# Weight stream in half chunks, and output banks emptied by units of their own, in a two-block fp32 transformer kernel

## The chip, the core and the metric

One core of a Trainium2 chip runs the whole program. Its engines work side by side, each through its own queue in order: TensorE (PE) multiplies, with weight loads (PEld) that overlap; VectorE (DVE) and ScalarE (ACT) work on SBUF and on the eight PSUM banks into which PE writes; GpSimd (POOL) does a little; SyncE (SP) issues the DMAs that bring weights from HBM. The metric is the device time of one execution in microseconds (us), lower is better.

## What is computed

Two layers of block 1 and two of block 2 on 256 tokens of width 1024, batch 1, all in float32. The reference, cut (in block 1 the attention is a differential one and a block one side by side; with 256 tokens the block one is plain causal attention):

```python
    for i in range(DEPTH):                      # block 1, DEPTH = 2
        h = rms_norm(x, ln_attn_g[i])
        dq, dk, dv, mq, mk, mv = jnp.split(h @ w_in[i], cuts, axis=-1)
        ...
        x = x + jnp.concatenate([y_diff, y_moba], axis=-1) @ w_out[i]
        x = x + conv_ffn(rms_norm(x, ln_ffn_g[i]), w_up[i], conv_w[i], conv_b[i], w_down[i])

def conv_ffn(h, w_up, conv_w, conv_b, w_down):
    u = causal_dwconv(h @ w_up, conv_w, conv_b)
    g, up = jnp.split(u, 2, axis=-1)
    return (jax.nn.silu(g) * up) @ w_down

    for l in range(L):                          # block 2, L = 2
        x = x + 0.5 * swiglu(rms_norm_2(x, ffn1_norm[l]), ffn1_w_gate[l], ffn1_w_up[l], ffn1_w_down[l])
        h = rms_norm_2(x, mix_norm[l])
        proj = h @ w_in[l] + b_in[l]
        q, k, v, f_logit, xr, gr, g_attn, g_rnn = jnp.split(proj, SPLIT_POINTS, axis=-1)
        ...
        y_attn = forgetting_attention(q, k, v, log_f) @ w_o_attn[l]
        xr = causal_depthwise_conv(xr, conv_w[l], conv_b[l])
        yr = rg_lru(xr, lru_w_a[l], lru_b_a[l], lru_w_x[l], lru_b_x[l], lru_lambda[l]) * jax.nn.gelu(gr)
        y_rnn = yr @ w_o_rnn[l]
        merged = jax.nn.sigmoid(g_attn) * y_attn + jax.nn.sigmoid(g_rnn) * y_rnn
        x = x + merged @ w_out[l]
        x = x + 0.5 * swiglu(rms_norm_2(x, ffn2_norm[l]), ffn2_w_gate[l], ffn2_w_up[l], ffn2_w_down[l])
```

The hidden width of every FFN is 2816, which is 22 tiles of 128.

## The kernel before

**Arithmetic.** A float32 value is split into a high part (a copy rounded to the multiplier's float32r) and a low part (the rest), and a product is made of high x high, low x high and high x low. Activations are kept transposed, 128 features by 256 tokens, with the high and the low part side by side in one tile of 512 columns. `mm2` is thus a pair of matmuls: the high weights against all 512 columns, and the low weights against the 256 high ones, added onto the first half of the same bank. An output tile fills one bank, whose two halves (`hi`, `lo`) are added when it is emptied.

**Weight stream.** All weights come in one list of chunks in the order of use, mostly 1 MB each (128 x 2048). SP brings a chunk into one of `NRAW` = 3 raw buffers; ACT writes its high part `wh` and DVE its low part `wl`, in `NP` = 4 pieces of 128 x 512, into one of `RING` = 3 buffers. ACT or DVE waits with a new chunk's first piece until PE is done with the chunk that held the buffer. `fill` and `urgent` put these pieces between other work; `next_chunk` hands a finished chunk to the matmuls and sets `st["done"]`, from which `h_open` sees which buffers may be written.

**Order.** The program is straight-line, and each engine runs its instructions as they were emitted. After nearly every pair of matmuls the emitter calls `substep`, which puts in weight pieces and lets background work advance. Background work is a list of Python generators, called units: a unit does a step on ACT or DVE, names the tile that it waits for, and goes on once an `Estimate` of each engine's time says that the tile is there. Units spawned with `front=True` come first and may run further ahead of PE (`CAPF` 4500 against `CAP` 1400 ns). The estimate only sets the order; on the chip semaphores hold it.

**FFN.** `proj2` makes two output tiles (gate and up) from one chunk: 16 pairs of matmuls into two banks `mm`. The unit `evac_swiglu` or `evac_conv` empties them into a tile `u` (ACT copies one half of each bank, DVE adds the other), scales by the norm's `rstd`, does silu and product (the conv one also four DVE taps into `y`), and writes the split hidden tile `as`. `ffn_order` sets where the down matmuls come: groups of four hidden tiles, the first half of the outputs beside the ups with a lag (4 tiles for the conv FFN, 2 for swiglu), then the second half. A half's last group runs output by output, and each finished output goes to `boundary` (x is updated, its square is added up on POOL for the next norm).

**Mix 2** runs the steps of `MIX2`: projections q, k, v, x, a, n, the block-diagonal gates G, then r0 to r3, n2, n3 (from the normed input `hS`), A0 to A3 (attention output), R0 to R3 (recurrence output `sp`), O0 to O3. The recurrence is in `lru_unit` (ACT exp, square, ln, exp; DVE products and scans into `z`), one for each of four tiles. `gelu_unit` empties the banks of r0 to r3 with a bias into `ge`, waits until all four recurrences are done, and then makes gelu, the product with `z`, and the split `sp`. It stands behind the `lru_unit`s in the list. `ya_unit` and `yr_unit` empty the banks of A and R and multiply by the gates `sg`.

Of the kernel before, what the change touches and what calls it, by code (L numbers as in the profile page):

```python
# [25 lines left out]
NG = -(-NF // 4)  # L26
NBLK = 41
# [40 lines left out]
class Estimate:  # L68
# [9 lines left out]
    def key(self, x):  # L78

        w = self.wide.get(x.name)  # L80
        return x.name if w is None else (x.name, 4 * x.offset // w)

    def cost(self, eng, op, out, ins, kw):
# [12 lines left out]
        if eng == "pool":  # L96
            return 149.0 + 2.1 * w
# [47 lines left out]
def kernel(ctx: ExitStack, tc: tile.TileContext, t: dict):  # L145
# [34 lines left out]
    def phase_chunks():  # L180
        for l in range(L):
            wo = t["w_out"]
            at = {"dq0": 0, "dq1": 1, "mq0": 2, "mq1": 3, "dv0": 4, "mv0": 5}
            for step in MIX1.split():
                if step[1] == "o":
                    stream.append(wo[l, 2 * (step[0] == "m") + int(step[2])])
                else:
                    stream.extend(t["w_p1"][l, at[step], i] for i in range(2))
            ffn_chunks(t["w_up"], t["w_down"], l, 4)
        for l in range(L):  # L190
# [3 lines left out]
            for step in MIX2.split():  # L194
                if step == "q0":
                    stream.append(t["w_qf"][l])
                elif step == "G":
                    stream.append(t["w_g"][l])
                elif step in PAIRS:
                    stream.extend(t["w_p2"][l, PAIRS.index(step), i] for i in range(2))  # L200
                elif step[0] == "O":
                    stream.append(half_rows(t["w_out2"][l], *divmod(int(step[1]), 2)))
                elif step[0] in "AR":
                    stream.append(t[{"A": "w_oa", "R": "w_or"}[step[0]]][l, int(step[1])])
                else:
                    stream.append(wi[l, base[step[0]] + int(step[1])])
            ffn_chunks(t["w_gu2"], t["w_d2"], l, 2)

    def half_rows(w, half, g):

        v = w[2 * g:min(2 * g + 2, w.shape[0])].rearrange("c p (k m) -> p c k m", k=2)
        return v[:, :, :, half * 512:(half + 1) * 512]

    def ffn_order(lag):
# [3 lines left out]
        for j in range(NF):  # L218
            yield "up", j
            while left and 4 * left[0] + 3 + lag <= j:  # L220
                yield "dn", (0, left.pop(0))
        for g in left:
            yield "dn", (0, g)
        for g in [NG - 1, *range(NG - 1)]:
            yield "dn", (1, g)

    def ffn_chunks(u, d, l, lag):
        for what, j in ffn_order(lag):
            stream.append(u[l, j] if what == "up" else half_rows(d[l], *j))
# [10 lines left out]
    NRAW = 3  # L240
    RING = 3
    NP = 4
# [7 lines left out]
    def issue_dma(parts=1, also=None):  # L250
# [16 lines left out]
        T["dma"] = max(T["dma"], T["dve"] if c >= NRAW else 0.0) + 2900.0  # L267
# [7 lines left out]
    def piece_h():  # L275
        c, p = divmod(st["h"], NP)
        if p == 0:
            Hs[c] = wpool.tile([P, wide(c)], F32R, tag="wh", bufs=RING, name=nm("wh"))
            Ls[c] = wpool.tile([P, wide(c)], F32R, tag="wl", bufs=RING, name=nm("wl"))
            est.wide[Hs[c].name] = est.wide[Ls[c].name] = wide(c)  # L280
# [18 lines left out]
    def fill():  # L299

        issue_dma()
        while h_open() and st["h"] - st["l"] < 2 * NP:
# [9 lines left out]
    def urgent():  # L312

        if st["l"] < min((st["use"] + 1) * NP, NCHUNK * NP):
# [88 lines left out]
    for x in X:  # L403
        est.wide[x.name] = 4 * S
# [7 lines left out]
    for c in range(2):  # L412
        issue_dma(NP, lambda i: i % 2 == 0 and nc.sync.dma_start(X[2 * c + i // 2], t["x"][2 * c + i // 2]))
    for p in range(4):
        est.R[X[p].name, 0] = est.R[X[p].name, 1] = T0 - 500.0 + 2200.0 * p
    est.R[raws[0].name], est.R[raws[1].name], T["dma"] = T0 + 200.0, T0 + 4600.0, T0 + 5500.0
    nc.sync.dma_start(cst, t["cst"])
    T["dma"] += 1400.0
    issue_dma()
# [25 lines left out]
    def mm3(out, lh, ll, rh, rl, start, stop):  # L445
        pe.matmul(out, lh, rh, start=start, stop=False, skip_group_check=True)
        pe.matmul(out, lh, rl, start=False, stop=False, skip_group_check=True)
        pe.matmul(out, ll, rh, start=False, stop=stop, skip_group_check=True)

# [108 lines left out]

    def mm2(b, lh, ll, x, start, stop):
# [4 lines left out]
    def proj2(R):  # L564

        h, l_ = next_chunk(None)
        h3 = h.rearrange("p (k c) -> p k c", k=KT)
        l3 = l_.rearrange("p (k c) -> p k c", k=KT)
        wait_for(lambda: bank_any(2))
        bs = [bank("mm") for _ in range(2)]  # L570
        for k in range(KT):
            for m in range(2):
                ms = slice(m * P, (m + 1) * P)
                mm2(bs[m], h3[:, k, ms], l3[:, k, ms], R.both(k), k == 0, k == KT - 1)
# [4 lines left out]
    def add_parts(t, bs):  # L579

        yield W("act", *bs)
        for m in range(2):
            act.activation(as2(t)[:, m], lo(bs[m]), AF.Copy)
        yield W("dve", t)
        for m in range(2):
            dve.tensor_add(as2(t)[:, m], hi(bs[m]), as2(t)[:, m])
            unbank()

    def add_bias(t, bs, cols):

        yield W("act", *bs)
        for m in range(2):
            act.activation(as2(t)[:, m], hi(bs[m]), AF.Identity, bias=cols[m])
        yield W("dve", t)
        for m in range(2):
            dve.tensor_add(as2(t)[:, m], lo(bs[m]), as2(t)[:, m])
            unbank()

    def vproj(R):

        h, l_ = next_chunk(None)
        h3 = h.rearrange("p (k c) -> p k c", k=KT)
        l3 = l_.rearrange("p (k c) -> p k c", k=KT)
        w = h3.shape[2]
# [4 lines left out]
        for k in range(KT):  # L609
            for m in range(2):  # L610
                ms = slice(m * P, (m + 1) * P)
                mm3(o[m], R.high(k)[:, ms], R.low(k)[:, ms], h3[:, k], l3[:, k],
# [5 lines left out]
    def vpair(R):  # L618
# [3 lines left out]
        for half in range(2):  # L622
            h, l_ = next_chunk(None)
            h3 = h.rearrange("p (k c) -> p k c", k=KT // 2)
            l3 = l_.rearrange("p (k c) -> p k c", k=KT // 2)
            for kk in range(KT // 2):
                k = half * (KT // 2) + kk
                for tt in range(2):
                    xh, xl = R.high(k)[:, tt * P:(tt + 1) * P], R.low(k)[:, tt * P:(tt + 1) * P]
                    last = k == KT - 1  # L630
                    pe.matmul(bs[tt], xh, h3[:, kk], start=k == 0, stop=False, skip_group_check=True)
                    substep()
                    pe.matmul(bs[tt], xl, h3[:, kk], start=False, stop=False, skip_group_check=True)
                    pe.matmul(bs[tt], xh, l3[:, kk], start=False, stop=last, skip_group_check=True)
                    if not (last and tt):
                        substep()
        return bs

    def down(acc, R, first, last, after=None):

        h, l_ = next_chunk(None)
        h3 = h.rearrange("p (k c) -> p k c", k=2)
        l3 = l_.rearrange("p (k c) -> p k c", k=2)

        def one(k, m):
            ms = slice(m * P, (m + 1) * P)
            mm3(as2(acc[m // 2])[:, m % 2], h3[:, k, ms], l3[:, k, ms], R.high(k), R.low(k),
                first and k == 0 and m % 2 == 0, last and k == 1 and m % 2 == 1)

        if not last:  # L650
            for k in range(2):
                for mh in range(2):
                    for m in range(4 * mh, 4 * mh + 4):
                        one(k, m)
                        substep()
        else:
            for p in range(4):
                for k in range(2):
                    for m in (2 * p, 2 * p + 1):
                        one(k, m)  # L660
# [6 lines left out]
    def down2(acc, R, ks, half_, first, last, after):  # L667

        h, l_ = next_chunk(None)
# [44 lines left out]
    def ffn(N, evac, scale, N2, lag, mul):  # L714
# [3 lines left out]
        for what, j in ffn_order(lag):  # L718
            if what == "up":
                spawn(evac(N, mul(R), j, A.tiles))  # L720
                substep()
            else:
                half_, g = j
                ks = range(4 * g, min(4 * g + 4, NF))
                wait_for(lambda: all(A.tiles[k] is not None for k in ks))
# [4 lines left out]
                down2(acc[half_], A, ks, half_, first, g == NG - 1 - half_, boundary(scale, N2))  # L730
# [10 lines left out]
    def evac_swiglu(N, bs, j, tiles):  # L741
        u = blk("u")
        yield from add_parts(u, bs)
        while N.rstd is None:
            yield POLL
        yield W("dve", u, N.rstd)
# [7 lines left out]
    def make_evac_conv(l):  # L754
        def evac(N, bs, j, tiles):
            u = blk("u")
            yield from add_parts(u, bs)
            while N.rstd is None:
                yield POLL
            yield W("dve", u, N.rstd)  # L760
# [21 lines left out]

    class Box:
        def __init__(self):
            self.ready = False
# [515 lines left out]
    def xr_unit(b, j, l, R):  # L1301

        x2 = blk("xr")
        yield from add_bias(x2, b, [v1(("bin", l), 24 + 2 * j + m) for m in range(2)])
# [39 lines left out]
    def sig_unit(b, cols, box, ready):  # L1344

        box.s = blk("sg")
        yield from add_bias(box.s, b, cols)
        while not ready():
            yield POLL
        yield W("act", box.s)  # L1350
# [323 lines left out]
```

## Time and profile before

| what | value |
|---|---|
| median of 3 runs (lowest to highest) | 1907.61 us (1906.86 to 1914.71) |
| the profiled execution: its time, its span | 1908.4 us, 1906.6 us |
| busy: PE, PEld, DVE, ACT, POOL | 97%, 85%, 81%, 67%, 4% |
| chain that ended last: PE, DVE, ACT, DMA | 89%, 4%, 4%, 2% |
| weights and data read from HBM | 336 MB, 177 GB/s over the span |

A matmul's end is modelled, and matmuls overlap, so the starts are to be read, not the lengths. A pair of `proj2` begins every 0.35 us. Where PE waits, the trace prints the wait in brackets with the instruction that ended it. The granted clock of a stretch (PEclk) is 1.00 at 2.4 GHz and 0.50 at 1.2 GHz. Since PE is at work for nearly the whole span, time can come from its waits, and from the stretches after them in which the clock is lower.

### The profile page before, as it was taken

How to read it: one execution, taken by the hardware profiler on the slowest of the kernel's cores; microseconds unless marked ns; L12 is line 12 of the kernel's file. 1: busy time of each engine (PE TensorE's matmuls, PEld its weight loads, DVE VectorE, ACT ScalarE, POOL GpSimd, SP SyncE). 2: the span in 40 equal slices, each digit the busy share in tenths (PEclk: the TensorE clock that was granted, in tenths of full speed). 3: DMA queues.
4: the chain of work that ended last, by engine and by line, in shares of the span. 5: the costliest groups of instructions: out<-in, count | busy, mean ns of one | idle time of the engine just before them, and what ended most of it. 6: DMA issues, size and time to landing. Idle time of an engine off the chain costs nothing.

```text
span 1906.6 us, 29974 instructions
## 1 busy us (share of the span) xinstructions
PE 1854.1 (97%) x10742; PEld 1618.0 (85%) x10742; DVE 1551.5 (81%) x3389; ACT 1283.8 (67%) x3211; POOL 68.9 (4%) x98
## 2 busy tenths in 40 slices
PE   8899999999999999999998999999999999899999
PEld 6788788888888888888887888888889888788888
DVE  6889997887989777778978977678777897888775
ACT  6777675877766665567787665566556778866653
POOL 3000000001000100000000100010001000000000
PEclk9999999999999999999999999999999999899999
DMA  9435455434545655474454555455556454455543
GB/s 260 142 128 181 173 172 204 147 124 163 181 160 166 209 193 185 153 258 164 145 192 168 190 182 193 164 199 192 198 169 241 155 177 162 169 180 199 193 159 132
DMA packets 79156, 339.59 MB, mean 178 GB/s; under 512 B 7020, under 2 KB 8084, under 8 KB 48288
## 3 DMA queue, kind: packets, MB, share of 16 engines
q1 hardware_dynamic: 77408, 330.20, 51.3%
q0 software_dynamic: 1456, 7.47, 1.4%
q8 instruction: 84, 1.38, 0.3%
q14 instruction: 64, 0.52, 0.1%
q10 hardware_dynamic: 144, 0.02, 0.0%
HBM read 336.30 MB, written 1.36 MB: 177 GB/s over the span
## 4 chain that ended last, share of the span: by engine, by line
PE 89%; DVE 4%; ACT 4%; DMA 2%; issue 1%; SPq 0%; ACTq 0%
PE mm L112 50%; PE acc L112 23%; PE mv L112 12%; DMA raw<-in_w_p 2%; DVE wl L112 2%; PE av L112 1%; ACT wh L112 1%; PE s L112 1%; PE qt L112 1%; PE pt L112 1%; DVE y L112 1%; ACT r L112 1%; ACT th L112 1%; DVE z L112 0%; DVE yc L112 0%
## 5 line engine op out<-in xcount | busy, mean ns | idle before, releaser
L112 DVE TENSOR_TENSOR wl<-raw,wh 128x512 fp32r<-128x512 f32 x1272 | 812.6, 679 | 142.3 <-ACT wh L112 133.0
L112 ACT ACTIVATE wh<-raw 128x512 fp32r<-128x512 f32 x1272 | 701.0, 618 | 146.4 <-PE acc L112 85.4
L112 PE MATMUL mm<-xs,wh 128*128 128x512 f32 x2112 | 742.6, 396 | 11.4 <-ACT as L112 8.4
L112 PE MATMUL mm<-xs,wl 128*128 128x256 f32 x2112 | 592.5, 281 | 0.0
L112 PEld LDWEIGHTS mm<-xs,wh 128*128 128x128 f32 x2112 | 397.7, 188 | 104.3 <-ACT as L112 9.0
L112 PEld LDWEIGHTS mm<-xs,wl 128*128 128x128 f32 x2112 | 401.0, 190 | 0.2
L112 PE MATMUL acc<-as,wh 128*128 128x512 f32 x1056 | 372.3, 396 | 6.6 <-DVE as L112 6.5
L112 PE MATMUL acc<-as,wl 128*128 128x256 f32 x1056 | 297.0, 281 | 0.0
L112 PE MATMUL mv<-wh,xs 128*128 128x512 f32 (+2 forms) x832 | 255.1, 384 | 0.2 <-ACT wh L112 0.2
L112 PEld LDWEIGHTS acc<-as,wh 128*128 128x128 f32 x1056 | 199.5, 189 | 53.1 <-DVE as L112 7.9
L112 ACT ACTIVATE u<-mm 128x256 f32<-128x256 f32 x264 | 95.5, 383 | 171.3 <-PE mm L112 171.1
L112 PEld LDWEIGHTS acc<-as,wl 128*128 128x128 f32 x1056 | 201.2, 191 | 0.0
L112 PE MATMUL mm<-hS,wh 128*128 128x512 f32 x512 | 184.2, 403 | 16.7 <-DVE ge L112 16.7
L112 DVE TENSOR_TENSOR u<-mm,u 128x256 f32<-128x256 f32 x264 | 100.4, 422 | 102.7 <-ACT u L112 102.6
L112 PEld LDWEIGHTS mv<-wh,xs 128*128 128x128 f32 x832 | 149.5, 189 | 26.8 <-ACT wh L112 0.7
L112 PE MATMUL mv<-wl,xs 128*128 128x512 f32 (+2 forms) x416 | 156.3, 376 | 0.2 <-DVE wl L112 0.2
L112 PE MATMUL mm<-hS,wl 128*128 128x256 f32 x512 | 144.4, 282 | 0.0
L112 PEld LDWEIGHTS mm<-hS,wh 128*128 128x128 f32 x512 | 98.0, 191 | 39.7 <-issue 17.3
L112 POOL TENSOR_TENSOR sq<-sq,sq 128x256 f32<-128x256 f32 x70 | 55.7, 796 | 1592.6 <-ACT sq L112 1590.8
L112 PEld LDWEIGHTS mm<-hS,wl 128*128 128x128 f32 x512 | 98.2, 192 | 0.1
L112 ACT ACTIVATE as<-u 128x256 fp32r<-128x256 f32 x88 | 36.3, 417 | 82.2 <-DVE u L112 82.2
L112 DVE TENSOR_TENSOR u<-u,rstd 128x512 f32<-128x512 f32 x132 | 90.3, 686 | 0.0
(208 smaller groups left out, 2262.8 us busy)
## 6 DMA issues: line engine op xcount, KB each, us to landing
raw<-in_w_gu SPq DMA_DIRECT2D x88, 1024.0 KB, 4.9
raw<-in_w_up SPq DMA_DIRECT2D x44, 1024.0 KB, 4.8
raw<-in_w_d SPq DMA_DIRECT2D x88, 512.0 KB, 4.8
raw<-in_w_p SPq DMA_DIRECT2D x42, 1024.0 KB, 5.1
raw<-in_w_in SPq DMA_DIRECT2D x34, 1024.0 KB, 4.8
raw<-in_w_down SPq DMA_DIRECT2D x44, 512.0 KB, 4.6
raw<-in_w_out SPq DMA_DIRECT2D x8, 1024.0 KB, 4.8
raw<-in_w_oa SPq DMA_DIRECT2D x8, 1024.0 KB, 4.9
```

The costliest lines, as they stand in the source:

```text
L112: f(*a, **k)
```

## The change

The list `stream` holds half chunks of 128 x 1024 (512 KB). A piece is still 128 x 512, so a half has two (`NP` 2). There are 7 raw buffers of a half and 5 buffers of converted halves, in place of 3 and 3 whole ones. `k_chunks` hands the halves to the matmuls one after another. Down groups have two hidden tiles, one half chunk each; the last two of the second half of the outputs run together. `urgent` looks two halves ahead.

A new unit, `summed`, empties the two banks of a `proj2` as its first and only step and is spawned with `front=True`; `evac_swiglu`, `evac_conv`, `xr_unit`, `sig_unit`, `gelu_unit`, `ya_unit` and `yr_unit` start from its tile in place of the banks. The bias is added by ACT to the half that ACT reads. The seven additions of squares of the first norm run on DVE, not on POOL. POOL's cost in the estimate changes, and the x tiles, the constants and the first raw halves are issued in another mix at the start. The matmuls are the same in number and shape.

```diff
-NG = -(-NF // 4)
-NBLK = 41
+NG = NF // 2
+NBLK = 43
...
-            return 149.0 + 2.1 * w
+            return 738.0 + 1.22 * w
         if op == "reciprocal":
             return 69.0 + 6.25 * w
...
         for j in range(NF):
             yield "up", j
-            while left and 4 * left[0] + 3 + lag <= j:
-                yield "dn", (0, left.pop(0))
+            while left and 2 * left[0] + 1 + lag <= j:
+                yield "dn", (0, (left.pop(0),))
         for g in left:
-            yield "dn", (0, g)
-        for g in [NG - 1, *range(NG - 1)]:
-            yield "dn", (1, g)
+            yield "dn", (0, (g,))
+        for g in range(NG - 2):
+            yield "dn", (1, (g,))
+        yield "dn", (1, (NG - 2, NG - 1))
...
-    NRAW = 3
-    RING = 3
-    NP = 4
+    NRAW = 7
+    RING = 5
+    NP = 2
...
-        if len(stream[c].shape) == 4:
-            rv = r.rearrange("p (c k m) -> p c k m", k=2, m=512)
-            for i in range(rv.shape[1]):
-                nc.sync.dma_start(rv[:, i], stream[c][:, i])
+        if len(stream[c].shape) == 3:
+            nc.sync.dma_start(r.rearrange("p (k m) -> p k m", k=2), stream[c])
         else:
             for i in range(parts):
                 if also:
                     also(i)
                 nc.sync.dma_start(r[:, i * w:(i + 1) * w], stream[c][:, i * w:(i + 1) * w])
-        T["dma"] = max(T["dma"], T["dve"] if c >= NRAW else 0.0) + 2900.0
+        T["dma"] = max(T["dma"], T["dve"] if c >= NRAW else 0.0) + 1450.0
         est.R[r.name] = T["dma"] + 2200.0
         return True
...
 
-        if st["l"] < min((st["use"] + 1) * NP, NCHUNK * NP):
+        if st["l"] < min((st["use"] + 2) * NP, NCHUNK * NP):
...
         else:
-            pool.tensor_add(N.ss[0], N.ss[0], sq)
+            (dve if N is norms[0] else pool).tensor_add(N.ss[0], N.ss[0], sq)
             N.ss = (N.ss[0], N.ss[1] + 1)
 
...
 
+    def k_chunks(n=KT, c=2):
+
+        per = n // c
+        for i in range(c):
+            h, l_ = next_chunk(None)
+            h3 = h.rearrange("p (k c) -> p k c", k=per)
+            l3 = l_.rearrange("p (k c) -> p k c", k=per)
+            for j in range(per):
+                yield i * per + j, h3[:, j], l3[:, j]
...
+    def summed(name, bs, cols=None):
+
+        x = Box()
+        x.t = blk(name)
+
+        def unit():
+            yield W("act", *bs)
+            for m in range(2):
+                if cols is None:
+                    act.activation(as2(x.t)[:, m], lo(bs[m]), AF.Copy)
+                else:
+                    act.activation(as2(x.t)[:, m], lo(bs[m]), AF.Identity, bias=cols[m])
+            yield W("dve", x.t)
+            for m in range(2):
+                dve.tensor_add(as2(x.t)[:, m], hi(bs[m]), as2(x.t)[:, m])
+                unbank()
+            x.ready = True
+
+        spawn(unit(), front=True)
+        return x
...
-    def down2(acc, R, ks, half_, first, last, after):
-
-        h, l_ = next_chunk(None)
-        h3 = h.rearrange("p (k c) -> p k c", c=512)
-        l3 = l_.rearrange("p (k c) -> p k c", c=512)
-
-        def one(i, m):
+    def down2(acc, R, groups, half_, first, last, after):
+
+        n = 2 * len(groups)
+
+        def one(i, m, h, l_):
             ms = slice(m * P, (m + 1) * P)
-            mm2(acc[m], h3[:, i, ms], l3[:, i, ms], R.both(ks[i]), first and i == 0, last and i == len(ks) - 1)
+            mm2(acc[m], h[:, ms], l_[:, ms], R.both(2 * groups[i // 2] + i % 2), first and i == 0, last and i == n - 1)
 
         if not last:
-            for i in range(len(ks)):
+            for i, h, l_ in k_chunks(n, len(groups)):
                 for m in range(4):
-                    one(i, m)
+                    one(i, m, h, l_)
                     substep()
         else:
+            w = list(k_chunks(n, len(groups)))
             for m in range(4):
-                for i in range(len(ks)):
-                    one(i, m)
-                    if i < len(ks) - 1:
+                for i, h, l_ in w:
+                    one(i, m, h, l_)
+                    if i < n - 1:
...
-    def gelu_unit(b, j, l, R):
-        ge = blk("ge")
-        yield from add_bias(ge, b, [v1(("bin", l), 32 + 2 * j + m) for m in range(2)])
-        while R.nh < 4:
-            yield POLL
+    def gelu_unit(x, j, l, R):
+        while not x.ready or R.nh < 4:
+            yield POLL
+        ge = x.t
         yield W("act", ge, R.h[j])
         fn(ge, ge, AF.Gelu_apprx_tanh)
         yield W("dve", ge)
```

Units `evac_swiglu`, `evac_conv`, `xr_unit`, `sig_unit`, `ya_unit` and `yr_unit` change as `gelu_unit` does.

ACT's order in the first layer of block 2, from the end of the gates to r3 (`ge<-mm` empties a bank of r0 to r3; `th<-th` are the ln and exp of a recurrence; `wh` is a weight piece). Before:

```order
L112 ACTIVATE wh_11068<-raw_10908 128x512 x4
L112 ACTIVATE th_10813<-th_10813,tiny 128x512
L112 ACTIVATE th_10813<-th_10813 128x512
L112 ACTIVATE th_10835<-th_10835,tiny 128x512
L112 ACTIVATE th_10835<-th_10835 128x512
L112 ACTIVATE wh_11119<-raw_10971 128x512 x4
L112 ACTIVATE th_10865<-th_10865,tiny 128x512
L112 ACTIVATE th_10865<-th_10865 128x512
L112 ACTIVATE ge_10952<-mm_10888,vec 128x256
L112 ACTIVATE ge_10952<-mm_10889,vec 128x256
L112 ACTIVATE ge_11006<-mm_10953,vec 128x256
L112 ACTIVATE ge_11006<-mm_10954,vec 128x256
```

The same place after the change:

```order
L112 ACTIVATE wh_11486<-raw_11246 128x512 x2
L112 ACTIVATE th_11425<-r_11424,sp_105 128x256 x2
L112 ACTIVATE wh_11509<-raw_11283 128x512
L112 ACTIVATE ge_11514<-mm_11448,vec 128x256
L112 ACTIVATE ge_11514<-mm_11449,vec 128x256
L112 ACTIVATE wh_11509<-raw_11283 128x512
L112 ACTIVATE th_11467<-r_11466,sp_105 128x256 x2
L112 ACT_TABLE_LOAD
L112 ACTIVATE r_11372<-r_11372,sp_105 128x256 x2
L112 ACTIVATE z_11544<-r_11372 128x512
L112 ACTIVATE wh_11552<-raw_11309 128x512 x2
L112 ACTIVATE ge_11574<-mm_11518,vec 128x256
```

The first bank of r0 is emptied ahead of the table load and the recurrence's exp, where it stood behind three recurrences' ln and exp.

DVE's order at the same layer's A steps and the start of R0 (`ya<-mm` empties the banks of an A step, `sp<-ge` makes the input of R0). Before, where A0's banks come behind all of `sp`:

```order
L112 TENSOR_TENSOR sp_11281<-ge_11063,sp_11281 128x256
L112 TENSOR_TENSOR sp_11315<-ge_11063,sp_11315 128x256
L112 TENSOR_TENSOR sp_11286<-ge_11118,sp_11286 128x256
L112 TENSOR_TENSOR sp_11321<-ge_11118,sp_11321 128x256
L112 TENSOR_TENSOR sg_11273<-mm_11209,sg_11273 128x256
L112 TENSOR_TENSOR sg_11273<-mm_11210,sg_11273 128x256
L112 TENSOR_TENSOR wl_11297<-raw_11129,wh_11296 128x512 x4
L112 TENSOR_TENSOR ya_11338<-mm_11276,ya_11338 128x256
L112 TENSOR_TENSOR ya_11338<-mm_11277,ya_11338 128x256
```

After the change, where the banks are those of A3, directly ahead of R0:

```order
L112 TENSOR_TENSOR sp_12061<-ge_11574,sp_12061 128x256
L112 TENSOR_TENSOR sp_12072<-ge_11574,sp_12072 128x256
L112 TENSOR_TENSOR ya_12079<-mm_12010,ya_12079 128x256
L112 TENSOR_TENSOR ya_12079<-mm_12011,ya_12079 128x256
L112 TENSOR_TENSOR ge_11637<-ge_11637,z_11633 128x512
L112 TENSOR_TENSOR ge_11696<-ge_11696,z_11686 128x512
L112 TENSOR_TENSOR sg_11047<-ya_12007,sg_11047 128x512
L112 TENSOR_TENSOR sg_11236<-ya_12079,sg_11236 128x512
L112 TENSOR_TENSOR sp_12088<-ge_11637,sp_12088 128x256
L112 TENSOR_TENSOR sp_12091<-ge_11637,sp_12091 128x256
```

The last four `sp` moved from ahead of A0's banks to behind A3's banks and four products.

DVE's order in the first conv FFN, at the eleventh up (`u<-mm` empties its banks, `y<-u` are taps of the convolution). Before:

```order
L112 SCALAR_TENSOR_TENSOR y_2432<-u_2353,vec,y_2432 128x254
L112 TENSOR_TENSOR wl_2427<-raw_2317,wh_2426 128x512 x4
L112 TENSOR_TENSOR as_2484<-y_2409,as_2484 128x256
L112 TENSOR_TENSOR y_2432<-y_2432 128x256
L112 TENSOR_TENSOR u_2418<-mm_2354,u_2418 128x256
L112 TENSOR_TENSOR u_2418<-mm_2355,u_2418 128x256
L112 TENSOR_TENSOR u_2476<-mm_2421,u_2476 128x256
L112 TENSOR_TENSOR u_2476<-mm_2422,u_2476 128x256
```

After:

```order
L112 SCALAR_TENSOR_TENSOR y_2606<-u_2471,vec,y_2606 128x255
L112 SCALAR_TENSOR_TENSOR y_2606<-u_2471,vec,y_2606 128x254
L112 SCALAR_TENSOR_TENSOR y_2606<-u_2471,vec,y_2606 128x255
L112 SCALAR_TENSOR_TENSOR y_2606<-u_2471,vec,y_2606 128x254
L112 TENSOR_TENSOR u_2631<-mm_2565,u_2631 128x256
L112 TENSOR_TENSOR u_2631<-mm_2566,u_2631 128x256
L112 TENSOR_TENSOR wl_2571<-raw_2418,wh_2570 128x512 x2
L112 TENSOR_TENSOR wl_2598<-raw_2450,wh_2597 128x512 x2
```

The banks of the up are emptied ahead of the weight pieces and one up at a time, where two ups' banks were emptied behind four pieces.

## Rows read from the trace of the kernel before

**Rows 1.** The profile's page: span, and busy time of each engine.

```profile
span 1906.6 us, 29974 instructions
PE 1854.1 (97%) x10742; PEld 1618.0 (85%) x10742; DVE 1551.5 (81%) x3389; ACT 1283.8 (67%) x3211; POOL 68.9 (4%) x98
```

**Rows 2.** PE's waits: for what; us in total, times, longest us.

```profile
PE mm L112 <- DVE ge L112: 16.7, 2, 8.4
PE qt L112 <- DVE qn L112: 9.5, 1, 9.5
PE mm L112 <- ACT as L112: 8.4, 2, 4.2
PE acc L112 <- DVE as L112: 6.5, 2, 3.3
PE mm L112 <- ACT wh L112: 2.0, 2, 1.0
PE st L112 <- POOL sq L112: 1.3, 1, 1.3
```

**Rows 3.** Windows: stretch and length, busy us of each engine, PEclk, DMA share, GB/s.

```profile
142.40:301.90 159.50, 150.54 (x854) 131.00 (x852) 149.07 (x314) 111.75 (x249) 2.35 (x3) 0.99 0.52 172
651.00:812.00 161.00, 161.00 (x930) 142.07 (x929) 124.21 (x247) 100.53 (x223) 4.31 (x6) 1.00 0.53 177
...
1600.00:1650.00 50.00, 41.64 (x243) 36.70 (x242) 34.57 (x66) 44.35 (x94) 0.00 (x0) 0.90 0.43 147
...
1012.20:1025.00 12.80, 12.80 (x65) 11.14 (x66) 10.77 (x24) 10.27 (x21) 0.00 (x0) 0.87 0.16 48
...
212.00:218.00 6.00, 5.00 (x19) 4.30 (x20) 5.83 (x14) 2.55 (x6) 0.00 (x0) 0.72 0.50 175
...
302.00:308.00 6.00, 6.00 (x25) 5.18 (x26) 5.81 (x13) 4.18 (x10) 1.49 (x2) 0.72 0.55 176
```

**Rows 4.** Timeline of PE between r3 and n2: start, length, instruction, [idle before].

```profile
1002.96 0.40 PE L112 MATMUL mm<-hS,wh 128*128 128x512 f32 x1
...
1003.31 0.40 PE L112 MATMUL mm<-hS,wh 128*128 128x512 f32 x1
...
1012.19 0.76 PE L112 MATMUL mm<-hS,wh 128*128 128x512 f32 x1 [8.37 <-DVE ge L112]
```

**Rows 5.** Timeline of ACT at the same place: the banks of r0 to r3.

```profile
1007.27 3.01 ACT L112 ACTIVATE ge<-mm,vec 128x256 f32<-128x256 f32 x8
```

**Rows 6.** DVE's groups from 975 to 1060 us: busy us, mean ns | idle before.

```profile
L112 DVE TENSOR_TENSOR ya<-mm,ya 128x256 f32<-128x256 f32 x8 | 3.0, 423 | 3.2 <-ACT ya L112 3.2
L112 DVE TENSOR_TENSOR sp<-ge,sp 128x256 fp32r<-128x256 f32 x8 | 2.9, 421 | 0.8 <-ACT sp L112 0.8
L112 DVE TENSOR_TENSOR sg<-ya,sg 128x512 f32<-128x512 f32 x4 | 2.7, 686 | 0.0
...
L112 DVE TENSOR_TENSOR ge<-ge,z 128x512 f32<-128x512 f32 x4 | 2.6, 685 | 0.0
```

**Rows 7.** Timeline of ACT at the start, at the end of its wait.

```profile
49.74 2.19 ACT L112 ACTIVATE wh<-raw 128x512 fp32r<-128x512 f32 x4 [6.70 <-DMA raw<-in_w_p]
```

**Rows 8.** Windows at the start, columns as in rows 3.

```profile
45.00:50.00 5.00, 0.00 (x0) 0.00 (x0) 0.00 (x0) 0.26 (x1) 0.00 (x0) 0.63 1.02 228
50.00:55.00 5.00, 2.35 (x9) 1.98 (x10) 4.59 (x10) 2.70 (x6) 0.00 (x0) 0.50 1.00 272
```

**Rows 9.** The page's DMA issues: KB each, us from issue to landing.

```profile
raw<-in_w_gu SPq DMA_DIRECT2D x88, 1024.0 KB, 4.9
...
raw<-in_w_d SPq DMA_DIRECT2D x88, 512.0 KB, 4.8
```

**Rows 10.** DVE's waits in the first conv FFN, 142 to 305 us, columns as in rows 2.

```profile
DVE y L112 <- ACT y L112: 7.8, 11, 3.1
```

**Rows 11.** Timeline of ACT at the wait in the first conv FFN.

```profile
208.72 1.67 ACT L112 ACTIVATE wh<-raw 128x512 fp32r<-128x512 f32 x3 [1.67 <-PE mm L112]
```

**Rows 12.** Timeline of ACT behind a swiglu FFN's last up.

```profile
795.59 0.73 ACT L112 ACTIVATE u<-mm 128x256 f32<-128x256 f32 x2 [1.63 <-PE mm L112]
```

**Rows 13.** Timeline of DVE there: the last hidden tile's low part.

```profile
799.54 0.42 DVE L112 TENSOR_TENSOR as<-u,as 128x256 fp32r<-128x256 f32 x1 [0.48 <-ACT as L112]
```

More of the change, by code (lines that the diff above doesn't have):

```diff
@@ L621, in vpair @@
         bs = [bank("mv") for _ in range(2)]
[L622 to L631, printed above, removed]
+        for k, h, l_ in k_chunks(c=4):
+            for tt in range(2):
+                xh, xl = R.high(k)[:, tt * P:(tt + 1) * P], R.low(k)[:, tt * P:(tt + 1) * P]
+                last = k == KT - 1
+                pe.matmul(bs[tt], xh, h, start=k == 0, stop=False, skip_group_check=True)
+                substep()
+                pe.matmul(bs[tt], xl, h, start=False, stop=False, skip_group_check=True)
+                pe.matmul(bs[tt], xh, l_, start=False, stop=last, skip_group_check=True)
+                if not (last and tt):
@@ L719, in ffn @@
             if what == "up":
-                spawn(evac(N, mul(R), j, A.tiles))
+                spawn(evac(N, summed("u", mul(R)), j, A.tiles))
                 substep()
             else:
-                half_, g = j
-                ks = range(4 * g, min(4 * g + 4, NF))
-                wait_for(lambda: all(A.tiles[k] is not None for k in ks))
+                half_, groups = j
+                wait_for(lambda: all(A.tiles[2 * g + i] is not None for g in groups for i in range(2)))
                 first = not acc[half_]
@@ L729, in ffn @@
                     acc[half_] = [bank("acc") for _ in range(4)]
-                down2(acc[half_], A, ks, half_, first, g == NG - 1 - half_, boundary(scale, N2))
+                down2(acc[half_], A, groups, half_, first, NG - 1 in groups, boundary(scale, N2))
     def finish_act(av, j, tiles):
@@ L739, in finish_act, with evac_swiglu @@
         tiles[j] = a
[L741 to L744, printed above, removed]
+    def evac_swiglu(N, x, j, tiles):
+        while not (x.ready and N.rstd is not None):
             yield POLL
+        u = x.t
         yield W("dve", u, N.rstd)
@@ L754, in make_evac_conv, with evac @@
     def make_evac_conv(l):
[L755 to L758, printed above, removed]
+        def evac(N, x, j, tiles):
+            while not (x.ready and N.rstd is not None):
                 yield POLL
+            u = x.t
             yield W("dve", u, N.rstd)
@@ L1299, in forget_unit, with xr_unit @@
         yield from split_out(b, out, m)
-    def xr_unit(b, j, l, R):
-        x2 = blk("xr")
-        yield from add_bias(x2, b, [v1(("bin", l), 24 + 2 * j + m) for m in range(2)])
+    def xr_unit(x, j, l, R):
+        while not x.ready:
+            yield POLL
+        x2 = x.t
         yield W("act", x2)
@@ L1342, in gate_unit, with sig_unit @@
         R.ng += 1
[L1344 to L1348, printed above, removed]
+    def sig_unit(x, box, ready):
+        while not (x.ready and ready()):
             yield POLL
+        box.s = x.t
         yield W("act", box.s)
@@ L1395, in split_pair, with ya_unit @@
             tiles[2 * j + m] = a
-    def ya_unit(b, sg, M, j):
-        u = blk("ya")
-        yield from add_parts(u, b)
-        while not sg.ready:
+    def ya_unit(x, sg, M, j):
+        while not (x.ready and sg.ready):
             yield POLL
+        u = x.t
         yield W("dve", u, sg.s)
@@ L1404, in ya_unit, with yr_unit @@
         M.t[j] = sg.s
-    def yr_unit(b, sg, M, j):
-        u = blk("yr")
-        yield from add_parts(u, b)
-        while M.t[j] is None or not sg.ready:
+    def yr_unit(x, sg, M, j):
+        while M.t[j] is None or not (x.ready and sg.ready):
             yield POLL
+        u = x.t
         yield W("dve", u, sg.s)
```

147 lines of the change are left out of this document (64 added, 83 removed).

## The prediction

> **What bounds the kernel now.** I read the page first: PE is busy for 1854.1 of 1906.6 us [rows 1], and the change leaves the matmuls alone. So all that it can gain is PE's idle time and the slower clock behind it, and all that it can lose is new idle time. Next come PE's waits, which name the places [rows 2]: 16.7 us in two waits for `ge` (one in each layer of mix 2), 9.5 once at the start, 8.4 in two waits in the conv FFNs, 6.5 in two more at their ends, and a few of 1 us. These six groups are 44.4 of the 52.5 us by which the span exceeds PE's busy time.
>
> A wait costs more than its length where the clock falls behind it. After the `ge` wait the granted clock is 0.87 over 12.8 us [rows 3], so 0.13 x 12.8 = 1.7 us of work is lost; the stretches behind a 4.2 us wait and a 3.3 us wait show 0.72 over 6 us, again 1.7 [rows 3]. The swiglu stretch without a wait shows 1.00 [rows 3]. So a `ge` wait is worth 8.4 + 1.7 = 10.1 us, a conv wait 4.2 + 1.7 = 5.9, the one at a conv FFN's end 3.25 + 1.7 = 4.9.
>
> **The change part by part.**
>
> *Banks of r0 to r3.* PE stops after r3 at 1003.5 and starts n2 at 1012.19 [rows 4], because n2 needs a bank and the eight banks of r0 to r3 are read by ACT only from 1007.27 on, all eight in one row [rows 5]; DVE's additions come behind that. After the change ACT reads each pair right behind its projection, ahead of the table load and the exps (the first order above), so n2 finds r0's banks two projections old. Both waits go: -2 x 10.1 = -20.2 us. If ACT ran late through the recurrences, which it fills nearly (44.35 of 50 us in the second layer [rows 3]), some would stay; I allow half, so -20 to -10.
>
> *R0.* The recurrence's steps now run beside the A steps, and the last four `sp` stand behind A3's banks (the second order). Behind the end of A3 DVE needs two `ya` at 0.42, two `ge` products and two `sg` products at 0.69, and one `sp` at 0.42 [rows 6]: 0.84 + 1.38 + 1.38 + 0.42 = 4.0, and some 0.4 for ACT's copy ahead (estimate). R0's first half chunk covers 8 pairs at 0.35 [rows 4], 2.8. A new wait of 4.4 - 2.8 = 1.6 us, twice: +3.2. Waits of 1 us in rows 2 are too short to be told apart in the clock, so none is added. Bounds: 0 if DVE has run ahead, 5 each with the clock if it lags: 0 to +10.
>
> *Start.* PE waits 9.5 us for `qn`, which waits for weight pieces, and these for a transfer that lands only at 49.74 [rows 7], with all 16 DMA engines busy (share 1.02 and 1.00 [rows 8]). What is late is bytes. The needed half chunk ends 0.5 MB sooner than the needed whole one: at 228 to 272 GB/s [rows 8] 1.9 to 2.3 us. The squares on DVE can take away up to the 1.3 us that PE waited for POOL [rows 2]. I take -3; bounds -6 (both, and the earlier bias tables) and +5 (a tenth of the 50 us, if smaller transfers carried a tenth less; see the rivals).
>
> *Conv FFNs.* The wait in the middle arises when ACT stands 1.67 us before a weight piece whose buffer PE still holds [rows 11], and the banks of two ups are emptied late. In the new order an up's banks are emptied alone and ahead of the pieces (the third order), so this wait goes: -5.9 each. But DVE is busy for 149.07 of the 159.5 us of this stretch [rows 3], and loses none of this work. What it did not do in the middle it must do before the last hidden tile: the conv taps of three ups stand behind the last up in the new order, some 14 us of rows of 0.42 to 0.69, against 4.2 us of PE work up to the first of these tiles and 1.7 more up to the last. That makes waits of 4 + 4 us, with the clock 8 + 2 x 1.7 = 11.4, for the 4.9 of before: +6.5. By this the part is +0.6 each. The other bound is DVE's own: the stretch can shrink by what DVE idles, 10.4 us, of which 7.8 are waits for ACT's `y` and 3.1 of these the wait in the middle [rows 10]: -3.1 each. I take -1 each, -2; bounds -7 to +6.
>
> *Swiglu FFNs, four.* The last up's hidden tile takes from 795.59 [rows 12] to 799.54 + 0.42 [rows 13] = 4.4 us. PE has a down group in between, 16 pairs or 5.5 us, and no wait (clock 1.00, PE busy for all of 161 [rows 3]). With groups of two tiles the cover is 8 pairs and the first pair of the last group, 3.2 us. A wait of 1.2 each: +4.8. Bounds 0 (the front unit shortens the chain) and +10.
>
> *Stage ends.* The last group of a half reads two half chunks at once in `down2`, so `st["done"]` counts the first as free while all four outputs still read it. ACT may then stand before a piece whose buffer is held, ahead of norm work queued behind it, and DVE behind ACT. No row of before has this at a stage's end; the nearest are the 1.67 us of rows 11 and PE's 1.0 us waits for `wh` [rows 2]. In the order after I find such a knot, six instructions of ACT and of DVE between two matmuls, at the start of both conv FFNs, and smaller ones ahead of three norms. I take 1.0 at each of five: +5; bounds 0 and 3 at ten places.
>
> *Others.* The DMAs are twice as many at half the size; outside the start the share is 0.43 to 0.52 [rows 3] and the stream runs ahead, so they hide: 0. The conversions have the same pieces. POOL's seven additions go to DVE at the start, where DVE waits for transfers anyway.
>
> **A rule that speaks against it.** The 512 KB transfers that the kernel already has land in 4.8 us, the 1024 KB ones in 4.9 [rows 9], at a DMA share of half. The Trainium skill ("DMA: Bandwidth & Descriptors", section "Bandwidth") asks for transfers of 1 MiB or more to get three quarters of the peak; by that, halves would cost rate. Where the stream has slack this changes nothing; by that rule the start alone would get longer, and its result is the third rival.
>
> **The sum.** -20.2 + 3.2 - 3 - 2 + 4.8 + 5 = -12.2 us. Against the profiled execution (span 1906.6, 1.8 around it, 1908.4) that is 1896.2; the median of the runs is 0.8 below that execution, so 1895.
>
> **The rivals.**
>
> *More of it is hidden.* The start gives 6, the conv FFNs -3 each, swiglu and the stage ends nothing: -20.2 + 3.2 - 6 - 6 = -29, about 1879. For it: the front units also shorten the chains at the tails. Against: DVE's load in the conv FFNs.
>
> *The wait moves to R0.* The recurrence must be done by R0 either way; before, the 8.4 us of idle time let ACT and DVE catch up. If they lag at A3, R0 waits 5 us and the clock falls: 2 x (5 + 1.7) = 13.4 in place of 3.2, so -2, about 1905. For it: ACT's 44.35 of 50. Against: before, the last `sp` was written ahead of A0's banks, four projections or some 22 us ahead of R0.
>
> *Small transfers slow the start.* If a tenth of the rate is lost in the first 50 us, +5 in place of -3: about 1903. For it: share 1.0 there and the rule above. Against: rows 9.
>
> *The buffers knot.* Five half chunks are 2.5 MB of converted weights, not 3, and are counted free too early at a half's last group. If ACT and DVE stand at every such place (six FFN ends, two mix 1 ends, two mix 2 ends) it costs ten times the price in place of the +5. Without the stage ends the sum is -17.2; it turns positive from 1.7 us at each place, and passes the bound for slower (+9.5) from 2.7. At 3 us: +13, about 1920. For it: the 1.67 us wait on ACT that became 4.2 on PE in the conv FFN. Against: there it met two full banks, and the new units empty these first.
>
> **How the numbers follow.** A measurement of this kernel can tell about 0.5%, 9.5 us, from no change: below 1898.1 is faster, above 1917.1 slower. Forecast 1895 (1889 to 1901): 0.44, of which 0.36 lies below 1898.1. More hidden 0.17. R0 0.20. Slow start 0.06. Knot 0.09. The rest 0.04, half faster, half the same. Faster 0.36 + 0.17 + 0.02 = 0.55; same 0.08 + 0.20 + 0.06 + 0.02 = 0.36; slower 0.09. The range reaches from the better rival to beyond R0's, 1879 to 1911; the knot and what is better still lie outside.
>
> **What would show it.** Right: no wait of PE for `ge`; one for `sp` of 1 to 2 us at R0, twice; the 4.2 us waits for `as` gone from the conv FFNs and longer or more waits of `acc` at their ends; four new waits of `acc` of about 1 us in the swiglu FFNs; `qt` waiting 6 to 7 us. Wrong: an `sp` wait of 5 us; a `qt` wait of over 10; waits of ACT's `wh` for `acc` at the stage ends that reach PE with over 2 us each; or a conv FFN stretch well under 156 us, which would mean that DVE's idle time there was not needed.

## The result, and the profile after

The changed kernel takes 1921.3 us (median of 6 runs, 1919.21 to 1923.26) against 1906.49 us of the kernel before (1902.75 to 1914.71): a ratio of 1.0075, 95% interval 1.0053 to 1.0097. It is slower by about 0.75%, where 1895 (1879 to 1911) was forecast. The time is outside the range and on the other side.

The page after, span and busy times, to be read against [rows 1]:

```profile
span 1920.6 us, 30794 instructions
PE 1868.9 (97%) x10742; PEld 1628.9 (85%) x10742; DVE 1562.8 (81%) x3372; ACT 1297.8 (68%) x3187; POOL 63.5 (3%) x91
```

PE's waits after, whole list, columns as in [rows 2]:

```profile
PE acc L112 <- DVE as L112: 16.2, 8, 3.8
PE st L112 <- POOL sq L112: 12.8, 7, 2.4
PE mm L112 <- DVE xs L112: 7.8, 6, 2.6
PE qt L112 <- DVE qn L112: 3.7, 2, 3.4
PE mm L112 <- DVE sp L112: 2.6, 2, 1.3
PE st L112 <- DVE sq L112: 2.3, 1, 2.3
PE warm L980 <- DVE vp L112: 2.0, 1, 2.0
PE mv L112 <- DVE xs L112: 0.4, 2, 0.2
```

The waits for `ge` and the waits of `mm` for `as` in the middle of the conv FFNs are gone, and the start is shorter (3.7 us against 9.5). In their place stand two groups that were small before: `acc` waits for `as`, 16.2 us (6.5 before), and PE waits for the next norm, `st` for POOL's `sq` and `mm` for `xs`, 20.6 us in 13 waits (before, 1.3 us for `sq` [rows 2] and twice 0.5 for `xs`). These 13 lie at the nine places where the program goes from one stage to the next.

The total of the waits has hardly moved (48.5 us before, 47.8 after), yet the span is 14.0 us longer. What grew is PE's busy time for the same matmuls: 1854.1 us before [rows 1], 1868.9 after, 14.8 more. The waits are now 29 in place of 17, at more places, and behind many of them the granted clock falls. Added up over windows of 6 us, busy time times what the clock lacks of 1.00 is some 11 us before and 19 after, about half of the 14.8; the rest was not traced.

What happens at these nine places is to be seen at the end of the second conv FFN. ACT's timeline of the changed kernel (start, length, instruction, [idle before <- what ended it]):

```profile
646.27 1.15 ACT L112 ACTIVATE wh<-raw 128x512 fp32r<-128x512 f32 x2 [1.62 <-PE acc L112]
651.16 1.15 ACT L112 ACTIVATE wh<-raw 128x512 fp32r<-128x512 f32 x2 [3.74 <-PE acc L112]
652.22 0.49 ACT L112 ACTIVATE xs<-x,vec 128x256 fp32r<-128x256 f32 x1
...
655.61 0.51 ACT L112 ACTIVATE xs<-x,vec 128x256 fp32r<-128x256 f32 x1 [1.45 <-DVE x L112]
```

DVE's at the same place:

```profile
648.15 0.87 DVE L112 TENSOR_TENSOR x<-acc,x 128x256 f32<-128x256 f32 x2
651.83 0.69 DVE L112 TENSOR_TENSOR wl<-raw,wh 128x512 fp32r<-128x512 f32 x1 [2.80 <-PE acc L112]
652.43 0.88 DVE L112 TENSOR_TENSOR x<-acc,x 128x256 f32<-128x256 f32 x2
...
655.89 0.88 DVE L112 TENSOR_TENSOR x<-acc,x 128x256 f32<-128x256 f32 x2
```

And POOL's last square with PE's wait for it:

```profile
657.76 0.81 POOL L112 TENSOR_TENSOR sq<-sq,sq 128x256 f32<-128x256 f32 x1 [0.45 <-ACT sq L112]
```

```profile
656.03 0.50 PE L112 MATMUL mm<-xs,wh 128*128 128x512 f32 x1 [0.61 <-DVE xs L112]
...
658.62 0.70 PE L112 MATMUL st<-sq,cst 128*128 128x256 f32 x2 [1.63 <-POOL sq L112]
```

A weight piece `wh` stands for 3.74 us in ACT's queue, until PE has read for the last time, in the step's last output, the buffer that the piece is to fill. Behind it wait the `xs` and `sq` of the next norm, the first of which need only an output that is done. DVE, whose `wl` is held up in the same way, stands for 2.80 us between the first and the second update of x. When both go on, PE is ending the step, and three of the last four outputs still go through x, `xs` and `sq` one behind the other in front of it. POOL is named as releaser of 12.8 us, but it only waits for ACT's `sq` in turn.

### The profile page after: what moved, and what is told of

Same layout as the page of the kernel before. It is cut to its first block, busy times and chain, and to the rows that moved or that the text cites. A ratio compares the mean times of both kernels' runs of the same rounds, so it can differ in the third digit from the quotient of the medians.

```text
span 1920.6 us, 30794 instructions
## 1 busy us (share of the span) xinstructions
PE 1868.9 (97%) x10742; PEld 1628.9 (85%) x10742; DVE 1562.8 (81%) x3372; ACT 1297.8 (68%) x3187; POOL 63.5 (3%) x91
## 4 chain that ended last, share of the span: by engine, by line
PE 88%; DVE 7%; ACT 2%; DMA 1%; issue 1%; POOL 0%; POOLq 0%; SPq 0%; ACTq 0%
PE mm L112 48%; PE acc L112 22%; PE mv L112 12%; DVE wl L112 2%; PE av L112 2%; DMA raw<-in_w_p 1%; PE s L112 1%; ACT wh L112 1%; PE qt L112 1%; DVE x L112 1%; PE pt L112 1%; DVE y L112 1%; PE g L112 1%; DVE xs L112 1%; DVE z L112 0%
## 5 line engine op out<-in xcount | busy, mean ns | idle before, releaser
L112 ACT ACTIVATE wh<-raw 128x512 fp32r<-128x512 f32 x1248 | 717.3, 627 | 255.8 <-PE acc L112 92.2
L112 PE MATMUL acc<-as,wh 128*128 128x512 f32 x1056 | 379.9, 400 | 16.2 <-DVE as L112 16.2
L112 POOL TENSOR_TENSOR sq<-sq,sq 128x256 f32<-128x256 f32 x63 | 50.2, 798 | 1597.4 <-ACT sq L112 1596.1
L112 PEld LDWEIGHTS mv<-wl,xs 128*128 128x128 f32 x416 | 80.0, 192 | 14.8
```

Source lines behind the costliest of these rows:

```text
L112: f(*a, **k)
```

## The experiments

**Hold the first half chunk.** A step that runs output by output reads both its half chunks until its end, but fetching the second sets `st["done"]` to the second, and the emitter takes the first for free. The edit sets it back:

```diff
             w = list(k_chunks(2))
+            st["done"] = st["use"] - 2
...
             w = list(k_chunks(n, len(groups)))
+            st["done"] = st["use"] - len(groups)
```

> The changed kernel, but where a step reads two half chunks output by output, the first of them counts as free only when the step is emitted. Theory 1 (ACT stands before a weight piece whose buffer PE still holds, ahead of the norm's work): ACT's 3.7 us waits at the stage ends go, PE's waits for the norm's squares fall from 15.1 us to about 2 and for xs from 7.8 to under 2, and with the clock behind them the time falls by 20 to 28 us, to 1893 to 1901. Rival (the squares are late because of POOL, its cost in the estimate or the deeper look of urgent): those waits stay and the time is within 5 us of the changed kernel's 1921.

Measured: 1887.23 us (1883.46 to 1888.68), ratio to the kernel before 0.9885 (0.9863 to 0.9908). That is 34 us less than the changed kernel, more than the 20 to 28 expected. PE's line of the page, and its waits:

```profile
PE 1856.0 (98%) x10742; PEld 1620.2 (86%) x10742; DVE 1558.7 (83%) x3372; ACT 1297.7 (69%) x3187; POOL 63.4 (3%) x91
```

```profile
PE acc L112 <- DVE as L112: 16.5, 8, 3.8
...
PE qt L112 <- DVE qn L112: 2.6, 1, 2.6
...
PE st L112 <- DVE sq L112: 1.1, 1, 1.1
PE mm L112 <- DVE xs L112: 0.6, 2, 0.3
```

ACT's timeline at the end of the second conv FFN:

```profile
633.44 1.15 ACT L112 ACTIVATE wh<-raw 128x512 fp32r<-128x512 f32 x2 [1.62 <-PE acc L112]
636.23 0.51 ACT L112 ACTIVATE xs<-x,vec 128x256 fp32r<-128x256 f32 x1 [1.64 <-DVE x L112]
...
640.88 2.70 ACT L112 ACTIVATE wh<-raw 128x512 fp32r<-128x512 f32 x5
```

The piece that stood ahead of `xs` is emitted behind the norm's work, and the seven waits for POOL's squares are gone, though POOL, its cost in the estimate and `urgent` are as in the changed kernel. The knot at the stage ends is worth 34 us, more than the whole loss of the change, and the rival (POOL, the estimate, the deeper look) falls. Of the 34, 20.0 are the waits for `sq` of POOL and `xs` (20.6 to 0.6), and 12.9 are PE's busy time (1868.9 to 1856.0): behind seven of the nine places the granted clock falls in the changed kernel, and behind none of them here.

**A larger ring, the count left as it is.**

```diff
-    NRAW = 7
-    RING = 5
+    NRAW = 5
+    RING = 6
```

> The changed kernel with six buffers of converted halves in place of five (and five raw ones in place of seven), and the first half of a two-half step still counted free too early. If the early count is the cause, a larger ring only moves which piece stands before a held buffer, and ACT is blocked again at the stage ends: PE's waits for squares stay over 10 us in all and the time is 1913 to 1925. If a ring of 2.5 MB is merely too small against 3 MB before, the waits shrink to under 5 us and the time goes to 1887 to 1900.

Measured: 1924.72 us (1923.48 to 1929.67), ratio 1.0094 (1.0074 to 1.0113), no better than the changed kernel. ACT stands for the same 3.74 us at the same place:

```profile
656.96 1.15 ACT L112 ACTIVATE wh<-raw 128x512 fp32r<-128x512 f32 x2 [3.74 <-PE acc L112]
```

PE's waits, of which those for squares are 11.9 us, over the 10 expected:

```profile
PE st L112 <- POOL sq L112: 9.5, 5, 2.4
...
PE qt L112 <- DVE qn L112: 6.8, 1, 6.8
PE st L112 <- DVE sq L112: 2.4, 1, 2.4
```

So it is not that the ring is smaller than before. With five buffers as with six, the emitter fills it up to the buffer that it wrongly counts as free.

**Another order of the last down groups.** Behind the last up, groups of the second half of the outputs, which need old hidden tiles, come between those that need the newest:

```diff
         for g in left:
-            yield "dn", (0, (g,))
-        for g in range(NG - 2):
-            yield "dn", (1, (g,))
+            for _ in range(lag // 2):
+                yield "dn", (1, (right.pop(0),))
+            yield "dn", (0, (g,))
+        for g in right:
+            yield "dn", (1, (g,))
```

(`right` begins as the list of the groups 0 to `NG` - 3.)

> The changed kernel with another order of the down groups: behind the last up, groups of the second half of the outputs come between the last groups of the first half (one ahead of each in the swiglu FFNs, two ahead of each in the conv FFNs). Theory (the tail waits are missing cover): PE's 16.2 us of waits of acc for as fall under 3, and with the clock behind the conv ones the time falls by 16 to 22 us, to 1899 to 1905. Rival (DVE is the bound of the conv FFNs, so its backlog only waits elsewhere): the four swiglu waits of 1.0 go, but at least 8 us of waits stay in the conv FFNs, and the time falls by less than 10.

Measured: 1894.41 us (1892.68 to 1896.04), ratio 0.9923 (0.9899 to 0.9947), 27 us less than the changed kernel, more than the 16 to 22 expected. PE's waits:

```profile
PE st L112 <- POOL sq L112: 12.8, 7, 2.4
...
PE acc L112 <- DVE as L112: 1.3, 2, 0.7
```

The waits for squares and `xs` stay to the tenth; those for `as` fall from 16.2 to 1.3 us. DVE's backlog in the conv FFNs was no bound of the stage: PE needed other work for the while (in the conv FFNs two groups, 5.5 us, ahead of each late one; in the swiglu FFNs one), and such work was there.

**Both edits.**

> The changed kernel with both edits of the two runs above. If the two causes are independent, the gains add: 1873 to 1884, faster than the kernel before by 23 to 33 us. If the conv FFNs' backlog or the norm's chain is the same bound seen at two places, the gain is that of the larger edit alone, 1893 to 1901.

Measured: 1865.72 us (1861.09 to 1867.49), ratio 0.9772 (0.9748 to 0.9795). That is 56 us less than the changed kernel, where the two gains of 34 and 27 make 61: they add up nearly, so the causes are in the main independent. It is below the 1873 to 1884 expected, and beats the kernel before by 2.3%. Waits that are left:

```profile
PE qt L112 <- DVE qn L112: 4.6, 1, 4.6
...
PE st L112 <- DVE sq L112: 1.0, 1, 1.0
PE mm L112 <- DVE xs L112: 0.5, 2, 0.3
```

**The units alone.** The kernel before with `summed` and the units that start from its tile; whole chunks, groups of four and the rings of three stay.

> The kernel before (whole chunks, groups of four, rings of three) with the units that empty the banks alone. If these units are what gains, and half chunks what loses: no wait for ge, no wait of over 2 us in the middle of the conv FFNs, no wait for squares beyond that of the start, and 1882 to 1892. If the half chunks are needed for the order to close (finer pieces), waits for a bank stay and the time is above 1898.

Measured: 1884.36 us (1882.63 to 1889.1), ratio 0.9877 (0.9854 to 0.9901): the units are a gain of 1.2% by themselves. PE's waits:

```profile
PE acc L112 <- DVE as L112: 9.3, 6, 2.5
PE qt L112 <- DVE qn L112: 8.8, 1, 8.8
PE mm L112 <- ACT wh L112: 2.0, 2, 1.0
...
PE st L112 <- POOL sq L112: 1.2, 1, 1.2
PE mm L112 <- DVE xs L112: 1.0, 2, 0.5
```

No wait for `ge`, none in the middle of the conv FFNs, and at the stage ends only the short ones that the kernel before has too (`xs`, twice 0.5, and `wh`, twice 1.0); the one wait for squares is that of the start, which is nearly as long as before. The rest of the change, laid on top of these units, costs 37 us (1884 to 1921).

**Units, whole chunks and the other order of groups.** Of the kernel above, with one group of the second half ahead of each late group of the first.

> Whole chunks and groups of four with the units that empty the banks, and with groups of the second half of the outputs between the last groups of the first half. Measures what half chunks are worth once the other two causes are out: against e3_hold_tail (1865.7) it differs by them alone. If half chunks only shorten the start (qt waits 8.8 us with whole chunks, 4.6 with halves) it takes 1869 to 1875; if finer pieces also help elsewhere, over 1878; if they cost (twice the DMAs, more waits on buffers), under 1865.

Measured: 1868.54 us (1866.35 to 1872.19), ratio 0.9796 (0.9778 to 0.9815). Against the units alone the other order of groups is worth 16 us here; with half chunks it was 27. The ratio of half chunks with both edits is 0.9772, and the intervals overlap, so no gain or loss by half chunks can be told. Nor would it be theirs alone, as the expectation had it: the two kernels differ by the rest of the change too (the order of issues at the start, the squares on DVE, POOL's cost, `urgent`), and by one group or two ahead of a late one in the conv FFNs. PE's waits differ at the start in `qt`, and in two waits for `wh`,

```profile
PE qt L112 <- DVE qn L112: 7.0, 1, 7.0
PE mm L112 <- ACT wh L112: 2.0, 2, 1.0
```

against 4.6 and none in the kernel with both edits.

**How far `urgent` looks.** With both edits:

```diff
-        if st["l"] < min((st["use"] + 2) * NP, NCHUNK * NP):
+        if st["l"] < min((st["use"] + 1) * NP, NCHUNK * NP):
```

> e3_hold_tail with urgent looking one half chunk ahead as the text of the kernel before reads, not two. If the deeper look matters (pieces forced ahead of norm work), the time moves by more than 4 us; if it only names the same distance in halves, it stays within 1862 to 1870.

Measured: 1866.31 us (1865.81 to 1868.8), ratio 0.9787 (0.9769 to 0.9805): no difference that can be told. The waits do move: those for `sp` and `as` are gone, and six for `wl`, 3.9 us in all, stand in their place.

**Cover for R0.** With both edits, the projection n3 moves from ahead of A0 to behind A3:

```diff
-            "A0 A1 A2 A3 R0 R1 R2 R3 O0 O1 O2 O3")
+            "A0 A1 A2 A3 n3 R0 R1 R2 R3 O0 O1 O2 O3")
```

> e3_hold_tail with the projection n3 moved from ahead of A0 to between A3 and R0. It covers the chain of the last recurrence products: PE's two waits for sp (2.6 us) go, and the time falls by 2 to 4 us to 1862 to 1864. Rival: the gate of n3 is then late for the last R step, and a wait for its sg takes their place, no gain.

Measured: 1864.46 us (1861.17 to 1864.88), ratio 0.9769 (0.9753 to 0.9786), not to be told from both edits alone. The rival was right that nothing is gained, but no wait for `sg` took the place of the others:

```profile
PE mm L112 <- DVE sp L112: 2.1, 2, 1.1
```

The two waits for `sp` stay, a little shorter. The last products are emitted as late ahead of R0 as before, since the emitter lets background work run only so far ahead of PE; more cover moved them along. That this is the reason was not tried; that these two waits hang on the order of emission is seen in the run before, where they are gone.

## Why the prediction was wrong

By its own steps, in the order of the sum:

- **Banks of r0 to r3, -20.2: right in kind, its size not measured apart.** No wait for `ge` is left, and the stretch that had 41.63 of 50 us and a clock of 0.93 in the windows of the kernel before is full after (windows, columns as in [rows 3]):

```profile
1000.00:1050.00 50.00, 50.00 (x288) 43.91 (x287) 42.07 (x79) 43.84 (x89) 0.00 (x0) 1.00 0.60 190
```

- **R0, +3.2: right in kind and size.** Two waits for `sp`, 1.3 each, where 1.6 was worked out; the clock did not fall.
- **Start, -3: right in direction.** `qt` waits 3.7 in place of 9.5, and `st` 2.3 in place of 1.3, together -4.8. The start is shorter, and the third rival, that smaller transfers lengthen it, did not come. That the half chunks are what shortens it is not shown: `qt` waits 1.7 to 4.6 us in the kernels with seven raw half buffers and 7.0 to 9.5 in those with whole chunks, but 6.8 with half chunks and five raw buffers (the run with the larger ring). The page's DMA issues after, columns as in [rows 9]:

```profile
raw<-in_w_gu SPq DMA_DIRECT2D x176, 512.0 KB, 4.4
```

  A half lands in 4.4 us where a whole chunk took 4.9 [rows 9]. The Trainium skill ("DMA: Bandwidth & Descriptors", section "Bandwidth") asks for 1 MiB or more in a transfer to get three quarters of the peak. A cost of smaller ones does show here, in the share of the 16 DMA engines' span that the queue's packets took for the same bytes (packets, MB, share; before, then after; 51.2 to 51.6% in all kernels with whole chunks, 52.9 to 57.2% in all with halves), but PE's list after has no wait for a transfer:

```profile
q1 hardware_dynamic: 77408, 330.20, 51.3%
q1 hardware_dynamic: 111392, 330.21, 55.8%
```

- **Conv FFNs, -2: right in kind, near in size by luck.** The middle wait is gone, and two waits stand at the end, 3.8 and 2.3 us where 4 and 4 were worked out. The clock behind them cost more than the 1.7 each that was taken (three windows around them in the first layer):

```profile
286.00:291.00 5.00, 1.20 (x7) 0.85 (x6) 4.89 (x12) 3.05 (x8) 0.00 (x0) 0.81 0.33 105
291.00:297.00 6.00, 3.72 (x11) 2.83 (x11) 5.86 (x13) 2.38 (x6) 0.00 (x0) 0.50 0.42 115
297.00:303.00 6.00, 6.00 (x21) 5.09 (x21) 5.62 (x13) 2.96 (x9) 1.46 (x2) 0.52 0.73 235
```

  PE works for 3.72 and 6.00 us at half the clock, which loses 0.50 x 3.72 + 0.48 x 6.00 = 4.7 us. With 6.1 us of waits that is 10.8, for the 11.4 of the sum: two errors that cancel. The other order of groups, which takes these waits and the swiglu ones away, gains 27 us, where 2 x 10.8 and 4 x 1.0 make 25.6.
- **Swiglu FFNs, +4.8: right.** Four waits of 1.0 us, for 1.2.
- **Stage ends, +5: wrong, and this is the step that failed.** The mechanism was named, but its size was far off. The edit that takes it away is worth 34 us. Without this term the sum stood at -17.2, or about 1890; the kernel without the knot takes 1887. With 2.6, -4.8, 4.1 and 34 for R0, the start, the swiglu FFNs and the stage ends, and the terms for banks and conv FFNs as forecast, the sum is +13.7; measured is +14.8. The sign that the prediction gave for this came too: 20.6 us over nine places are 2.3 that reach PE at each.

Four things were mis-sized in that term. First, the price of one place: it was taken as 1.0, near the 1.0 us of PE's waits for `wh` [rows 2] and below ACT's 1.67 [rows 11]. But the 1.67 was the wait for a buffer that PE was about to leave, while a step that runs output by output holds its first half chunk to its last output. ACT waits 3.74 us there, and DVE 2.80; ACT's wait is 3.7 to 3.9 us at seven of the nine places, and 2.0 and 2.1 at the two behind mix 2, where the profile names no releaser but the edit takes PE's waits away as well. Second, the number of places: five were counted, by looking for six instructions of ACT and DVE between two matmuls. One weight piece that stands in the wrong place makes no such bunch; it is two rows among the others. There are nine stages that end in a norm, and at all nine PE waits. Third, what stands behind: the pieces block ACT and DVE at the head of a chain of eight updates, products and squares that PE waits for as a whole. Fourth, the clock: nothing was added for it, as waits of 1 us had not moved it, but these waits are longer, and 12.9 of the 34 us are PE's busy time.

Together, 34 us over nine places are 3.8 each. The fourth rival gave the rule for this: it turns the sum positive from 1.7 a place and slower from 2.7, and at 3 gives 1920. It had the right mechanism, ten places and nearly the right price, and got a chance of 0.09, on the argument that the units would empty the banks first. That argument is about banks; at a stage's end what is late is not a bank but the norm.

## What to carry to other kernels

When an in-order engine also fills a ring of buffers, look up for each kind of step how long the step holds its oldest buffer, not when the last one was fetched; a fill emitted too early costs the rest of that step and everything queued behind it, and the trace names an innocent last link (here POOL's squares) as the releaser. A finer grain of a weight stream is no gain by itself: here no gain of it could be told but perhaps a shorter start, and the same grain took away the cover of the newest tiles and broke a count that was right for whole chunks. Work that depends on nothing recent (here the other half of the outputs) belongs between the steps that need the newest results.

## What the runs showed of the hardware

The clock does not follow from the length of a wait alone. In the changed kernel each of the four swiglu FFNs of block 2 begins with two waits, of 0.6 and 1.6 us. Behind those of the first FFN of a layer (655 to 659 us and 1288 to 1291) the clock stays at 1.00; behind those of the second (1097 to 1101 and 1730 to 1734) it falls. The first FFN comes behind another FFN, the second behind mix 2 (windows of the changed kernel):

```profile
657.00:661.00 4.00, 2.38 (x13) 2.12 (x14) 3.73 (x6) 3.98 (x7) 1.11 (x2) 1.00 0.30 75
661.00:665.00 4.00, 4.00 (x25) 3.48 (x24) 2.87 (x7) 3.71 (x9) 0.00 (x0) 1.00 0.70 248
...
1099.00:1103.00 4.00, 2.38 (x10) 1.86 (x9) 3.82 (x6) 3.98 (x7) 1.29 (x2) 0.80 0.31 90
1103.00:1107.00 4.00, 4.00 (x20) 3.46 (x19) 2.66 (x7) 2.95 (x8) 0.00 (x0) 0.77 0.72 256
```

The windows 1289 to 1297 show 1.00, those from 1732 to 1740 show 0.61 and 0.96. What decides between the two is not settled by these runs. A wait of 2.0 us, at the start of the first mix 2 (847.45, with one of 0.2 some 3 us before it), was enough for a fall:

```profile
848.00:852.00 4.00, 4.00 (x23) 4.00 (x22) 2.65 (x5) 3.85 (x7) 0.00 (x0) 0.61 0.97 355
```

And two waits a few us apart kept the clock at 0.50 and 0.52 through 12 us (291 to 303, above), where behind the single wait of 3.3 us that ended at 301.27 in the kernel before it was 0.72 from 302 to 308 [rows 3] and 1.00 from 308 to 314.
